# Residual row scale and offset built on chip, first expert tile loaded in halves, router offset first

## The chip, the cores and the metric

One core of a Trainium2 chip. Its engines are TensorE (PE, with its weight loads PEld), VectorE (DVE), ScalarE (ACT), GpSimd (POOL) and SyncE (SP), which here only issues transfers. The metric is the device time of the one core in microseconds, lower is better. A profile of one execution stands beside the timed runs.

## What is computed

A transformer block on 256 tokens of 1024 features, all in float32. Attention (two kinds, gated and merged) is followed by a residual and a layer norm, then 32 experts of which every token uses 4, and a second residual and layer norm.

```python
x = layer_norm(DEEPNORM_ALPHA * x + mix, ln1_g[l], ln1_b[l])     # mix: the attention part
ffn = moe(x.reshape(B * S, D), w_router[l], b_router[l], w_mlp1[l], b_mlp1[l], w_mlp2[l], b_mlp2[l])
x = layer_norm(DEEPNORM_ALPHA * x + ffn.reshape(B, S, D), ln2_g[l], ln2_b[l])

def moe(x2, ...):
    logits = x2 @ w_router + b_router
    top_v, top_i = lax.top_k(logits, 4)
    gates = softmax(top_v)
    # each expert e, on the tokens that chose it
    h = xb @ w_mlp1[e] + b_mlp1[e]                       # 1024 -> 2048
    x_glu, x_lin = minimum(h[:, ::2], 7), clip(h[:, 1::2], -7, 7)
    y = x_glu * sigmoid(1.702 * x_glu) * (x_lin + 1) @ w_mlp2[e] + b_mlp2[e]
```

Every expert's weights are read from DRAM once: 8 MB of `w_mlp1` and 4 MB of `w_mlp2` for each of 32 experts, 402 MB of the 440 MB that the program moves.

## The kernel before, in words

The weights come as chunks of 1 MB, two to a unit. Units 0 to 13 are the attention's weights (28 chunks, `N1` = 28), units 14 to 205 the experts', six to an expert. `seq` is the order in which PE uses them: eight chunks of an expert's first matrix (`m1`), then four of the second matrix of the expert before it (`m2`). A unit lives in a 2 MB tile in SBUF; there are ten places: five of a ring, two of `spl`, one each of `ring4` and `ring3`, and one that is made of two separate 1 MB halves ("nh" and "xl"). SP issues all these loads in program order. When PE has used a chunk, `refill` gives the place to the next unit in `queue`: a 2 MB place is refilled after its second chunk by one transfer (`feed`), the halves one at a time after their own chunk (`feed_half`). Before the experts start, `feed` and `feed_half` fill all ten places while the attention finishes.

Between attention and experts stands the router, in a fixed order that the program writes out (`manual_schedule`): `residual`, `normal` (layer norm), `turn` (transposes of the normed rows to `x1T`), `logits` (eight matmuls with `wr` and one with the offset `br`), `choose` (top 4 on DVE), `count`, `place`, `pick`, then `gather`, which fetches the chosen tokens' rows with matmuls. The first expert chunk follows on PE. Everything later hangs on `at((kind, expert, chunk), f)`: f is issued behind that chunk on each engine that it uses. `combine(e)` adds expert e-2's result to the sums `Y` in PSUM and so frees the buffers "oh" and "ol"; `onehot(e)` spreads an expert's token numbers into the PSUM buffer "pv".

The second residual, ALPHA * x, is added to `Y` by PE: `x1_part` rebuilds x from the normed rows `xn` in quarters (t: half of the tokens, h: half of the features), first times `ln1_g` (j = 0), then plus `ln1_b` (j = 1), and `y_x1` multiplies the quarter by ALPHA times the identity (held in `lstrict` by then). To have g and b in all 128 rows, `x1_load` fetches both with two POOL transfers into the buffer "oh", and a matmul with a broadcast column of `ident` copies one row of it to all rows in "pv". The four quarters are done in experts 3 to 6.

Of the kernel before, what the change touches and what calls it, by code (L numbers as in the profile page):

```python
# [9 lines left out]
F32 = mybir.dt.float32  # L10
# [8 lines left out]
NE = 32  # L19
# [12 lines left out]
def block_kernel(ctx: ExitStack, tc: tile.TileContext, x, xT, w_in, cols_in, b_v, lam_v,  # L32
                 rpbx, w_da, w_na, w_out, ln1_g, ln1_b, w_router, b_router,
                 w1, b1, w2, b2, ln2_g, ln2_b, consts, out):
    nc = tc.nc
# [4 lines left out]
    pp = ctx.enter_context(tc.tile_pool(name="pp", bufs=1, space=bass.MemoryType.PSUM))  # L40

    def act(o, i, f=AF.Copy, **kw):
        return nc.scalar.activation(o, i, f, **kw)  # L43

    def tt(o, a, b, op):
        return nc.vector.tensor_tensor(out=o, in0=a, in1=b, op=op)  # L46
# [17 lines left out]
    N1 = len(chunks)  # L64

    def m1c(e, u):
        return w1[e, u * 256:(u + 1) * 256, :].rearrange("(p r) c -> p r c", p=128)

    def m2c(e, u):
        return w2[e, u * 512:(u + 1) * 512, :].rearrange("(p k) c -> p k c", p=128)  # L70
# [7 lines left out]
    queue = list(range((N1 + len(seq)) // 2))  # L78
    ring = {}
    home = {}  # L80
# [39 lines left out]
    def expert_unit(u):  # L120
        return seq[2 * u - N1]

    half = [None]
    lnt = []

    def feed_half(s):

        if s == 0:
            half[0] = queue.pop(0) if queue else None
        u = half[0]  # L130
        if u is None:
            return
        home[u] = "half"
        kind, e, c = expert_unit(u)
        t = ring[2 * u + s] = big.tile([128, 2048], F32, name="ring5", tag=("nh", "xl")[s])
        if kind == "m1":
            nc.sync.dma_start(t, m1c(e, c // 2)[:, s])
        else:
            nc.sync.dma_start(t.rearrange("p (k c) -> p k c", k=2), m2c(e, c // 2)[:, 2 * s:2 * s + 2])

    def refill(i):

        where = home[i // 2]
        if where == "half":
            feed_half(i % 2)
        elif i % 2:
            if not queue and where is not ring_tile and not lnt:
                load_ln2(where())
            else:
                feed(where)  # L150
# [26 lines left out]
    ident = keep.tile([128, 128], F32, name="ident")  # L177
    lstrict = keep.tile([128, 128], F32, name="lstrict")
    ones = keep.tile([128, 128], F32, name="ones")
# [6 lines left out]
    wr = keep.tile([128, 8, NE], F32, name="wr")  # L186
    br = keep.tile([1, 2, NE], F32, name="br")
# [16 lines left out]
    def at(key, f, *a):  # L204
        after.setdefault(key, []).append((f, a))
# [10 lines left out]
    binT, gcol, g1col, b1col = col[:, 0:40], col[:, 40:41], col[:, 41:49], col[:, 49:57]  # L216
# [10 lines left out]
    p = pp.tile([128, 512], F32, name="tp", bufs=1)  # L227
# [16 lines left out]
    for j in range(4):  # L244
        u, r = divmod(j, 2)
        v = ring[0][:, j * 512:(j + 1) * 512]
# [3 lines left out]
        s = slice(2 * j, 2 * j + 2)  # L250
# [321 lines left out]
    for i in range(N1):  # L572
        if i + 1 < N1:
            split(i + 1)
        if i < 20:
            (proj_v if i // 2 in (2, 5) else proj_t)(i)
        elif i < 24:
            branch(i)
        elif i < 26:
            outproj((i - 24,))  # L580
        elif i == 27:
            outproj((2, 3))
        refill(i)
        if i == N1 - 1:
            feed_half(1)
            for j in range(SPL):
                feed(spl_tile)
        run_after(i)
        if i == 18:

            p1_scope.close()
            p2 = ctx.enter_context(tc.tile_pool(name="p2", bufs=1))
            p2b = ctx.enter_context(tc.tile_pool(name="p2b", bufs=1))
            last = ctx.enter_context(tc.tile_pool(name="last", bufs=1))
            feed(lambda: last.tile([128, 4096], F32, name="ring4"))
        if i == 23:
            feed_half(0)
            feed(lambda: big.tile([128, 4096], F32, name="ring3", tag="qq"))
# [21 lines left out]
    def cut(h):  # L620
        return slice(h * 512, (h + 1) * 512)
# [15 lines left out]
    x1T = big.tile([128, 8, T], F32, name="x1T", tag="xh")  # L637
# [9 lines left out]
    def logits(t):  # L647

        pl = lgs[t] = pp.tile([128, 512], F32, name=("tp", "pv")[t], bufs=1)
        for k in range(8):  # L650
            nc.tensor.matmul(pl[:, 0:NE], lhsT=x1T[:, k, t * 128:(t + 1) * 128], rhs=wr[:, k], start=(k == 0), stop=False)
        nc.tensor.matmul(pl[:, 0:NE], lhsT=ones[0:1], rhs=br[:, 1], start=False, stop=True)

    m8s = {}

# [210 lines left out]

    x1p = []

    def x1_load():

        gb = p2b.tile([4, 512], F32, name="gb", tag="oh", bufs=1)
        for j, src in enumerate((ln1_g, ln1_b)):
            nc.gpsimd.dma_start(gb[2 * j:2 * j + 2], src.rearrange("(h n) -> h n", h=2))
        x1p[:] = [gb, p2b.tile([128, 512], F32, name="x1p", tag="ol", bufs=1)]

    def x1_part(t, h, j):

        p = pp.tile([128, 512], F32, name="pv", bufs=1)
        gb, v = x1p
        nc.tensor.matmul(p, lhsT=ident[0:4, 2 * j + h:2 * j + h + 1].to_broadcast([4, 128]), rhs=gb, start=True, stop=True)  # L880
        tt(v, v if j else xn[:, t, cut(h)], p, ALU.add if j else ALU.mult)

    def y_x1(t, h):

        nc.tensor.matmul(Y[t][:, h], lhsT=lstrict, rhs=x1p[1], start=False, stop=False, skip_group_check=True)  # L885

    yb = []

# [55 lines left out]
    at(("m1", 1, 1), lambda: nc.gpsimd.tensor_scalar(lstrict, ident, ALPHA, None, op0=ALU.mult))  # L944
    for e in range(4):
        t, h = divmod(e, 2)
        at(("m1", e + 3, 1), x1_load)
        at(("m1", e + 3, 3), x1_part, t, h, 0)
        at(("m1", e + 3, 4), x1_part, t, h, 1)
        at(("m1", e + 3, 6), y_x1, t, h)  # L950
    at(("m1", 1, 3), onehot, 0)
    at(("m1", 1, 1), activate, 0)
    at(("m1", 8, 3), y_bias_load)
# [7 lines left out]
    Y = [pp.tile([128, 2, 512], F32, name="pj", bufs=2) for t in range(2)]  # L961
# [5 lines left out]
    residual(1, 1)  # L967
    turn(0)
    logits(0)
    normal(1)  # L970
    choose(0)
    turn(1)
    logits(1)
    count(0)
    choose(1)
# [117 lines left out]
    for t, h in ((1, 1), (0, 0), (0, 1), (1, 0)):  # L1093
        v, y, m = fin[:, t, cut(h)], Y[t][:, h], mv[t]
# [71 lines left out]
```

## Time and profile before

| what | value |
|---|---|
| median of 3 timed runs | 1171.37 us (1169.43 to 1171.55) |
| the profiled execution | 1170.98 us, of which 1169.2 us are the span from its first to its last instruction |
| PE busy | 1085.4 us (93% of the span) |
| DVE, ACT, POOL busy | 369.6, 247.9, 25.2 us |
| mean granted TensorE clock | 0.980 |
| moved by transfers | 439.87 MB, mean 376 GB/s |

The span is told in stretches: up to about 200 us attention, then the router, and from 214 us on the experts. A mean over the span hides that these have different limits, so each sentence below that concerns a stretch uses that stretch's own rows. A PE that is "busy" may be running at half clock, which the column of the granted clock tells.

### The profile page before, as it was taken

The numbers are of one execution on the slowest core, as the hardware profiler recorded it, in microseconds if no ns is written. First come the engines' busy times: TensorE is split into PE (matmuls) and PEld (weight loads), VectorE is DVE, ScalarE is ACT, GpSimd is POOL, SyncE is SP. The second block draws the span as 40 slices with busy tenths as digits, with TensorE's granted clock in tenths as the row PEclk, the third lists the DMA queues.
The fourth block names the chain that finished last, engine by engine and source line by source line (L and its number), as shares of the span: only waits on it lengthen the run. The fifth ranks groups of instructions, "written<-read, shape, count | busy, mean of one in ns | idle before, by whom it ended". The sixth has DMA issues, their size and how long they took to land.

```text
span 1169.2 us, 13431 instructions
## 1 busy us (share of the span) xinstructions
PE 1085.4 (93%) x5592; PEld 522.1 (45%) x5592; DVE 369.6 (32%) x786; ACT 247.9 (21%) x487; POOL 25.2 (2%) x38
## 2 busy tenths in 40 slices
PE   9999999999999999999999999998988998999874
PEld 8887898543332333443433433333333333333221
DVE  6968756132112222222232222222222222222213
ACT  5466843311100111111111111111111111111011
POOL 0001100000000000000000000000000000000001
PEclk9999999899889999999999999999999999999997
DMA  9943469799998899999999999999999999999991
GB/s 337 378 169 113 167 227 369 313 427 426 408 383 354 339 371 411 428 426 427 428 426 428 426 428 425 427 429 427 428 426 425 430 428 426 427 427 429 427 407 51
DMA packets 51043, 439.87 MB, mean 376 GB/s; under 512 B 5906, under 2 KB 9106, under 8 KB 23714
## 3 DMA queue, kind: packets, MB, share of 16 engines
q1 hardware_dynamic: 50098, 437.86, 90.8%
q8 instruction: 46, 0.75, 0.3%
q0 software_dynamic: 592, 0.57, 0.2%
q10 hardware_dynamic: 288, 0.52, 0.1%
q14 instruction: 19, 0.16, 0.0%
HBM read 437.89 MB, written 1.05 MB: 375 GB/s over the span
## 4 chain that ended last, share of the span: by engine, by line
DMA 44%; PE 21%; issue 3%; POOL 0%; POOLq 0%; SPq 0%
DMA ring<-in_w_dram 42%; PE sc L796 10%; PE tp L841 6%; PE sc L815 1%; DMA gb<-in_ln_b_dram 1%; PE tp L731 1%; PE pj L864 1%; PE pv L731 1%; DMA ring<-in_ln_g_dram 0%; PE pv L880 0%; PE pv L760 0%; PE pj L903 0%; PE pj L885 0%; POOLq L1162 0%; POOL ring L1098 0%
## 5 line engine op out<-in xcount | busy, mean ns | idle before, releaser
L796 PE MATMUL sc<-ring,XS 128*64 128x512 f32 x2048 | 482.1, 608 | 33.5 <-DMA ring<-in_w_dram 33.0
L796 PEld LDWEIGHTS sc<-ring,XS 128*64 128x64 f32 x2048 | 138.4, 138 | 307.3 <-issue 254.9
L841 PE MATMUL tp<-ring,hsas 128*64 128x512 f32 x1024 | 234.9, 598 | 14.5 <-DMA ring<-in_w_dram 14.0
L841 PEld LDWEIGHTS tp<-ring,hsas 128*64 128x64 f32 x1024 | 69.1, 136 | 153.6 <-issue 122.5
L804 DVE COPY hsas<-sc 128x512 f32<-128x512 f32 x32 | 22.1, 692 | 310.5 <-PE sc L796 310.5
L43 ACT ACTIVATE XS<-tp,gbx 128x128 f32<-128x128 f32 x64 | 25.8, 453 | 416.7 <-PE tp L731 414.8
L284 PE MATMUL pj<-XH,sp 128*128 128x256 f32 x512 | 96.7, 288 | 4.0 <-DVE sp L46 3.7
L284 PEld LDWEIGHTS pj<-XH,sp 128*128 128x128 f32 x512 | 80.7, 192 | 8.5 <-DVE sp L46 4.9
L46 DVE TENSOR_TENSOR sp<-ring,sp 128x1024 fp32r<-128x1024 f32 (+1 forms) x58 | 68.1, 1188 | 26.9 <-ACT sp L43 26.7
L762 DVE TENSOR_SCALAR GT<-pv,slotp 128x256 fp32r<-128x256 f32 x32 | 15.5, 484 | 186.2 <-PE pv L760 186.2
L284 PE MATMUL pj<-XL,sp 128*128 128x256 f32 x256 | 73.1, 286 | 0.0
L43 ACT ACTIVATE sp<-ring 128x1024 fp32r<-128x1024 f32 (+1 forms) x58 | 58.0, 1023 | 66.9 <-PE pj L284 31.0
L46 DVE TENSOR_TENSOR gl<-sc,bT 128x512 f32<-128x512 f32 x62 | 42.6, 687 | 66.0 <-PE sc L815 66.0
L43 ACT ACTIVATE as<-gl 128x256 f32<-128x256 f32 x64 | 26.7, 416 | 153.7 <-DVE gl L822 153.7
L854 DVE SCALAR_TENSOR_TENSOR ol<-tp,GS,oh 128x512 fp32r<-128x512 f32 x32 | 24.0, 751 | 101.0 <-ACT oh L43 101.0
L284 PEld LDWEIGHTS pj<-XL,sp 128*128 128x128 f32 x256 | 49.2, 192 | 0.6 <-issue 0.6
L43 ACT ACTIVATE oh<-tp,GS 128x512 fp32r<-128x512 f32 x32 | 22.0, 687 | 112.4 <-PE tp L841 112.4
L731 PEld LDWEIGHTS tp<-P,xres 128*128 128x128 f32 x256 | 34.1, 204 | 26.1 <-issue 25.9
L815 PEld LDWEIGHTS sc<-ident,hsas 128*128 128x128 f32 x248 | 32.4, 210 | 25.2 <-issue 25.2
L43 ACT ACTIVATE hsas<-sc 128x512 f32<-128x512 f32 x32 | 19.1, 597 | 103.8 <-PE sc L796 103.8
L731 PE MATMUL tp<-P,xres 128*128 128x128 f32 x256 | 40.3, 303 | 0.1
L815 PE MATMUL sc<-ident,hsas 128*128 128x128 f32 x248 | 38.2, 297 | 0.0
(212 smaller groups left out, 768.3 us busy)
## 6 DMA issues: line engine op xcount, KB each, us to landing
ring<-in_w_dram SPq DMA_DIRECT2D x171, 2048.0 KB, 34.2
ring<-in_w_dram SPq DMA_DIRECT2D x42, 1024.0 KB, 31.9
ring<-in_w_in_dram SPq DMA_DIRECT2D x17, 1024.0 KB, 13.3
ring<-in_w_out_dram SPq DMA_DIRECT2D x4, 1024.0 KB, 6.7
ring<-in_w_in_dram SPq DMA_DIRECT2D x4, 512.0 KB, 7.7
nb<-in_rpbx_dram SPq DMA_DIRECT2D x8, 256.0 KB, 3.6
ring<-in_w_da_dram SPq DMA_DIRECT2D x2, 1024.0 KB, 5.1
ring<-in_w_na_dram SPq DMA_DIRECT2D x2, 1024.0 KB, 7.9
```

The costliest lines, as they stand in the source:

```text
L43: return nc.scalar.activation(o, i, f, **kw)
L46: return nc.vector.tensor_tensor(out=o, in0=a, in1=b, op=op)
L284: nc.tensor.matmul(pj[g][:, c], lhsT=a(k, cc), rhs=b[:, kk], start=(kk == 0 and j == 0 and c % 2 == 0), stop=(kk == 7 and j == 2), skip_gr ...
L731: nc.tensor.matmul(px[:, u], lhsT=v, rhs=P[g][:, t], start=(t == 0), stop=(t == 1))
L762: nc.vector.tensor_scalar(GT[e], p[:, 256:512], slotp[:, 0:1], None, op0=ALU.is_equal)
L796: nc.tensor.matmul(HP[h][j * CAP:(j + 1) * CAP], lhsT=XS[e // 2][:, c, e % 2], rhs=w[:, h, j], start=(c == 0), stop=(c == 7), skip_group_c ...
L804: nc.vector.tensor_copy(HS[e][:, 1], HP[1])
L815: nc.tensor.transpose(p[:, s, k], v[:, s, k], ident)
L841: nc.tensor.matmul(OP[e][j * CAP:(j + 1) * CAP], lhsT=AS[e][:, c, k], rhs=ring[i][:, n:n + 512], start=(c + k == 0), stop=(c == 3 and k == ...
L854: nc.vector.scalar_tensor_tensor(out=ol, in0=OP[e], scalar=GS[e], in1=oh.bitcast(F32), op0=ALU.mult, op1=ALU.subtract)
L864: nc.tensor.matmul(Y[t][:, j], lhsT=GT[e][r, t * 128:(t + 1) * 128], rhs=w[r], start=(e + n == 0), stop=False, skip_group_check=True)
```

## The change

Three edits. The residual's quarters move from experts 3 to 6 to experts 9 to 12, with other places inside the expert, and g and b reach all rows without transfers: ACT multiplies the identity by a column of g (or b) that has been in SBUF since the start, four times for 512 features, and a matmul with a matrix of ones sums each column of that diagonal. Unit 14, the first that the experts use, goes to the two halves instead of unit 18, which takes a full place. In the router the offset's matmul comes ahead of the eight others, and two matmuls of ones, whose result nobody reads, are put behind the first offset.

```diff
-    half = [None]
+    half = [N1 // 2]
+    queue.remove(N1 // 2)
...
-        if s == 0:
+        if s == 0 and N1 // 2 in home:
             half[0] = queue.pop(0) if queue else None
...
         pl = lgs[t] = pp.tile([128, 512], F32, name=("tp", "pv")[t], bufs=1)
+        nc.tensor.matmul(pl[:, 0:NE], lhsT=ones[0:1], rhs=br[:, 1], start=True, stop=False)
+        if t == 0:
+            keep_clock(2)
         for k in range(8):
-            nc.tensor.matmul(pl[:, 0:NE], lhsT=x1T[:, k, t * 128:(t + 1) * 128], rhs=wr[:, k], start=(k == 0), stop=False)
-        nc.tensor.matmul(pl[:, 0:NE], lhsT=ones[0:1], rhs=br[:, 1], start=False, stop=True)
+            nc.tensor.matmul(pl[:, 0:NE], lhsT=x1T[:, k, t * 128:(t + 1) * 128], rhs=wr[:, k], start=False, stop=(k == 7))
+
+    def keep_clock(n):
+
+        p = pp.tile([128, 512], F32, name="sc", bufs=2)
+        for j in range(n):
+            nc.tensor.matmul(p[:, 0:128], lhsT=ones, rhs=ones, start=True, stop=True)
...
-    def x1_load():
-
-        gb = p2b.tile([4, 512], F32, name="gb", tag="oh", bufs=1)
-        for j, src in enumerate((ln1_g, ln1_b)):
-            nc.gpsimd.dma_start(gb[2 * j:2 * j + 2], src.rearrange("(h n) -> h n", h=2))
-        x1p[:] = [gb, p2b.tile([128, 512], F32, name="x1p", tag="ol", bufs=1)]
-
     def x1_part(t, h, j):
 
+        gb = p2b.tile([128, 4, 128], F32, name="gb", tag="oh", bufs=1)
+        for k in range(4):
+            act(gb[:, k], ident, scale=(g1col, b1col)[j][:, 4 * h + k:4 * h + k + 1])
         p = pp.tile([128, 512], F32, name="pv", bufs=1)
-        gb, v = x1p
-        nc.tensor.matmul(p, lhsT=ident[0:4, 2 * j + h:2 * j + h + 1].to_broadcast([4, 128]), rhs=gb, start=True, stop=True)
+        nc.tensor.matmul(p, lhsT=ones, rhs=gb.rearrange("p k c -> p (k c)"), start=True, stop=True)
...
-        at(("m1", e + 3, 1), x1_load)
-        at(("m1", e + 3, 3), x1_part, t, h, 0)
-        at(("m1", e + 3, 4), x1_part, t, h, 1)
-        at(("m1", e + 3, 6), y_x1, t, h)
+        at(("m1", 9 + e, 2), x1_part, t, h, 0)
+        at(("m1", 9 + e, 4), x1_part, t, h, 1)
+        at(("m1", 9 + e, 6), y_x1, t, h)
```

PE in the first expert that has a quarter, expert 3 before. L796 are the expert's chunks (four rows each), L760 is `onehot`, L880 the copy of g or b to all rows, L731 `gather`, L885 `y_x1`:

```order
L796 MATMUL sc<-ring,XS 64x512 x8
L864 MATMUL pj<-oh,GT 128x512 x4
L864 MATMUL pj<-ol,GT 128x512 x4
L796 MATMUL sc<-ring,XS 64x512 x4
L760 MATMUL pv<-rows,stack 128x512
L796 MATMUL sc<-ring,XS 64x512 x4
L880 MATMUL pv<-gb,ident 128x512
L796 MATMUL sc<-ring_2415,XS 64x512 x4
L880 MATMUL pv<-gb,ident 128x512
L796 MATMUL sc<-ring_2415,XS 64x512 x4
```

The same place now, in expert 9 (L805 the chunks, L769 `onehot`, L884 the copy):

```order
L805 MATMUL sc<-ring,XS 64x512 x8
L873 MATMUL pj<-oh,GT 128x512 x4
L873 MATMUL pj<-ol,GT 128x512 x4
L805 MATMUL sc<-ring,XS 64x512 x4
L769 MATMUL pv<-rows,stack 128x512
L884 MATMUL pv<-gb,ones 128x512
L805 MATMUL sc<-ring,XS 64x512 x8
L884 MATMUL pv<-gb,ones 128x512
L805 MATMUL sc<-ring,XS 64x512 x4
```

The first copy has come forward by one chunk: it now stands right behind `onehot`, which writes the same buffer "pv"; the second keeps its place, two chunks behind the first instead of one. On ACT eight builds of "gb" stand between `gate_o` (oh) and the gather's evictions (XS) of each of these four experts:

```order
L43 ACTIVATE oh<-tp,GS 128x512
L43 ACTIVATE gb<-ident,col 128x128 x8
L43 ACTIVATE XS<-tp,gbx 128x128 x2
L43 ACTIVATE XS<-pv,gbx 128x128 x2
L43 ACTIVATE hsas<-sc 128x512
```

Before, ACT went there from `oh` to `XS` at once. In the router PE had, before (L644 `turn`, L651 the eight matmuls, L652 the offset, L680 and L679 `count`):

```order
L644 MATMUL sc<-ident,xres 128x128 x8
L651 MATMUL tp<-wr,x1T 128x32 x8
L652 MATMUL tp<-br,ones 128x32
L644 MATMUL sc<-ident,xres 128x128 x8
L651 MATMUL pv<-wr,x1T 128x32 x8
L652 MATMUL pv<-br,ones 128x32
L680 MATMUL sc<-maskM,lstrict 128x32
```

and has now (L651 the offset, L661 the two matmuls of ones, L655 the eight):

```order
L645 MATMUL sc<-ident,xres 128x128 x8
L651 MATMUL tp<-br,ones 128x32
L661 MATMUL sc<-ones 128x128 x2
L655 MATMUL tp<-wr,x1T 128x32 x8
L645 MATMUL sc<-ident,xres 128x128 x8
L651 MATMUL pv<-br,ones 128x32
L655 MATMUL pv<-wr,x1T 128x32 x8
L689 MATMUL sc<-maskM,lstrict 128x32
```

Each offset has moved ahead of its eight matmuls, and two matmuls stand between the first offset and the first eight.

## Rows read from the trace of the kernel before

**Rows 1.** Windows; stretch, its length, busy us by engine, granted clock, transfers' share, GB/s

```profile
230.00:300.00 70.00, 67.72 (x336) 27.19 (x330) 18.89 (x48) 10.50 (x23) 1.11 (x2) 1.00 1.01 426
300.00:440.00 140.00, 131.93 (x544) 47.45 (x546) 30.80 (x70) 14.91 (x32) 2.98 (x6) 0.90 0.92 368
440.00:600.00 160.00, 160.00 (x790) 63.98 (x788) 39.23 (x95) 23.50 (x50) 2.01 (x4) 1.00 1.01 424
600.00:800.00 200.00, 189.66 (x933) 75.32 (x931) 44.46 (x109) 27.70 (x60) 0.00 (x0) 1.00 1.01 428
```

**Rows 2.** Windows of 5 us in the same view, two of the stretch 300 to 440

```profile
350.00:355.00 5.00, 5.00 (x22) 1.36 (x18) 0.69 (x1) 0.60 (x1) 0.00 (x0) 1.00 0.21 52
...
420.00:425.00 5.00, 5.00 (x23) 1.76 (x22) 0.69 (x1) 0.60 (x1) 0.00 (x0) 1.00 0.82 279
```

**Rows 3.** Waits of PE; for whom, us in total, times, longest us

```profile
PE sc L796 <- DMA ring<-in_w_dram: 33.0, 30, 1.6
...
PE pv L880 <- DMA gb<-in_ln_b_dram: 10.0, 4, 2.7
```

**Rows 4.** Timeline of expert 3; start, length, instructions, [idle before, on whom]

```profile
295.69 0.49 PE L760 MATMUL pv<-rows,stack 96*128 96x512 f32 x1
...
296.23 0.48 DVE L762 TENSOR_SCALAR GT<-pv,slotp 128x256 fp32r<-128x256 f32 x1 [5.31 <-PE pv L760]
296.75 0.42 DVE L765 SCALAR_TENSOR_TENSOR as<-GT,pv 128x256 f32<-128x256 f32 x1
...
300.61 2.04 PE L880 MATMUL pv<-gb,ident 4*128 4x512 f32 x2 [2.55 <-DMA gb<-in_ln_b_dram]
302.58 3.68 PE L796 MATMUL sc<-ring,XS 128*64 128x512 f32 x8
...
307.63 1.94 PE L796 MATMUL sc<-ring,XS 128*64 128x512 f32 x8
```

**Rows 5.** Chain of work that ended last; start, length, what

```profile
408.25 1.09 PE pv L880 x2
...
419.73 1.05 PE pj L885 x2
...
514.93 1.13 PE pj L864 x8
...
540.93 1.13 PE pj L864 x8
...
615.54 35.57 DMA ring<-in_w_dram
```

**Rows 6.** Groups by line; busy us, mean ns of one, idle before

```profile
L43 ACT ACTIVATE XS<-tp,gbx 128x128 f32<-128x128 f32 x64 | 25.8, 453 | 416.7 <-PE tp L731 414.8 <-issue 1.7
```

**Rows 7.** Timeline of SP's issues at the start of the experts

```profile
219.32 7.52 SPq L113 DMA_DIRECT2D ring<-in_w_dram  x2
...
226.51 7.74 SPq L113 DMA_DIRECT2D ring<-in_w_dram  x3
```

**Rows 8.** Windows of 5 us at the router's end and the first chunks

```profile
210.00:215.00 5.00, 4.87 (x22) 3.62 (x24) 1.07 (x7) 1.58 (x6) 0.54 (x1) 0.52 1.01 433
215.00:220.00 5.00, 5.00 (x28) 2.44 (x25) 0.00 (x0) 0.80 (x2) 0.00 (x0) 1.00 0.07 30
225.00:230.00 5.00, 5.00 (x26) 1.66 (x24) 2.73 (x16) 3.61 (x8) 0.00 (x0) 1.00 0.73 246
```

**Rows 9.** Timeline of PE in the router and at the first gathers

```profile
202.66 1.97 PE L651 MATMUL tp<-wr,x1T 128*128 128x32 f32 x16 [0.31 <-ACT x1T L43]
...
208.18 0.63 PE L652 MATMUL pv<-br,ones 1*128 1x32 f32 x2
...
211.22 2.05 PE L731 MATMUL tp<-P,xres 128*128 128x128 f32 x8
...
213.86 2.41 PE L796 MATMUL sc<-ring,XS 128*64 128x512 f32 x8
...
216.20 1.21 PE L731 MATMUL pv<-P,xres 128*128 128x128 f32 x8
```

More of the change, by code (lines that the diff above doesn't have):

```diff
@@ L867, in block_kernel @@
     x1p = []
-    def x1_load():
-        gb = p2b.tile([4, 512], F32, name="gb", tag="oh", bufs=1)
-        for j, src in enumerate((ln1_g, ln1_b)):
-            nc.gpsimd.dma_start(gb[2 * j:2 * j + 2], src.rearrange("(h n) -> h n", h=2))
-        x1p[:] = [gb, p2b.tile([128, 512], F32, name="x1p", tag="ol", bufs=1)]
     def x1_part(t, h, j):
+        gb = p2b.tile([128, 4, 128], F32, name="gb", tag="oh", bufs=1)
+        for k in range(4):
+            act(gb[:, k], ident, scale=(g1col, b1col)[j][:, 4 * h + k:4 * h + k + 1])
         p = pp.tile([128, 512], F32, name="pv", bufs=1)
-        gb, v = x1p
-        nc.tensor.matmul(p, lhsT=ident[0:4, 2 * j + h:2 * j + h + 1].to_broadcast([4, 128]), rhs=gb, start=True, stop=True)
+        nc.tensor.matmul(p, lhsT=ones, rhs=gb.rearrange("p k c -> p (k c)"), start=True, stop=True)
+        if j == 0:
+            x1p[:] = [p2b.tile([128, 512], F32, name="x1p", tag="ol", bufs=1)]
+        v = x1p[0]
         tt(v, v if j else xn[:, t, cut(h)], p, ALU.add if j else ALU.mult)
     def y_x1(t, h):
-        nc.tensor.matmul(Y[t][:, h], lhsT=lstrict, rhs=x1p[1], start=False, stop=False, skip_group_check=True)
+        nc.tensor.matmul(Y[t][:, h], lhsT=lstrict, rhs=x1p[0], start=False, stop=False, skip_group_check=True)
     yb = []
```

## The prediction, made before the run

> **What bounds the kernel now.** I start with stretches, because the busy shares of the whole span mislead here: PE is 93% busy, yet it isn't PE alone that sets the end. From 230 to 300 us the transfers run at 426 GB/s, from 440 on at 424 and 428 [rows 1]; 427 is what this program gets when a load is always outstanding. Between 300 and 440 they make only 368, although 32 experts' weights are still waiting to be read, with windows as low as 52 GB/s [rows 1, 2]. The loads can't run ahead there: all ten places are full, and a place becomes free only when PE has used it. So in that stretch PE's delays turn into idle time of the transfers, and idle transfers are never made up, since from 440 to the end they run at their full rate.
>
> After 440 PE is ahead of what the transfers can follow. Two equal points of neighbouring experts are 540.93 - 514.93 = 26.0 us apart [rows 5]; an expert's 12 MB (12.58 million bytes) take 29.45 us at 427 GB/s. PE uses up the stock in the places, 3.45 us per expert, and PE's chain ends at 615.54, where its first wait for a weight begins [rows 5]. From there on the transfers alone set the time; PE's waits for weights (33.0 us at the expert's first matrix, 30 times, 1.6 at most) are theirs [rows 3].
>
> Why is PE late from 300 to 440? Its waits name one thing apart from weights: L880, the copy of g and b, 10.0 us in 4 waits [rows 3]. Expert 3 shows one. `onehot` and the next chunk are done by 298.1, then PE stands 2.55 us for the second POOL transfer, and after that it runs at half its speed: eight chunk matmuls take 3.68 us, later 1.94 again [rows 4]. From the first such copy (300.61) to the fourth (408.25) it is 107.6 us, 35.9 per expert [rows 4, 5], 9.9 more than 26.0: 2.5 of waiting, 3.2 of the quarter's own matmuls at full speed (1.09, as much again, and 1.05 for y_x1 [rows 5]) and about 4.2 of half clock.
>
> **Does this lag explain the lost transfer time?** By bytes the loss is 140 x (1 - 368/427) = 19.3 us. By the lag: places were last full at the release of 226.51 [rows 7]; until 295 PE gained 69 x (1 - 26.0/29.45) = 8 us of stock, then lost 4 x (35.9 - 29.45) = 25.8, so 17.8 us of idle. The two roads agree within 1.5 us. I take the bytes, since they are counted, and 17.8 to 19.6 (with 428) for the range.
>
> **The residual's quarters.** Removed are eight small POOL transfers and PE's four waits for them. With the quarters gone from experts 3 to 6, those experts cost 26.0 us like the later ones, less than the 29.45 of the transfers, so the transfers have no idle time left there: -19.3.
>
> What comes back in experts 9 to 12? Eight builds of a 128x128 tile on ACT: nothing of before builds from SBUF with a column as scale, the nearest is the gather's eviction, 128x128 with a column of scale and of offset, 0.45 us [rows 6]; nothing to 0.45 each, I take 0.45. Four make 1.8 us. They can start when `combine` has read "oh", and one chunk (1.94 [rows 4]), `onehot` and its DVE work lie beside them: hidden, and if that cover were gone, 1.8 us of PE wait per copy. Behind them on ACT stand only the gather's evictions, three chunks later. The matmul with ones has 512 columns as before and costs the same 1.09 as the copy from four rows; y_x1, which already has 128 rows, shows 1.05 [rows 5]. New is the wait behind `onehot`: the copy writes "pv", which DVE reads until 297.17, while `onehot` itself ended at 296.18 [rows 4], so PE stands 1.0 us. The second copy is two chunks on, past the DVE work, and waits for nothing.
>
> So such an expert takes 26.0 + 3.2 + 1.0 = 30.2 us, 0.8 more than the transfers need; even if each wait drew the same 4.2 us of half clock, 34.4. PE waited up to 1.6 us for weights [rows 3] and the windows from 440 to 800 still show the clock at 1.00 [rows 1], so I take 30.2. What covers it is the stock. Emptied from the last window below rate, 425 [rows 2], to 615.54 [rows 5], it is 190 x (1 - 26.0/29.45) = 22 us, less some 2 for the second matrix's offset in expert 8: about 20. In the new run it starts full at 226.5 and is empty near 410, so experts 9 to 12 may lose 20 us before a transfer idles. Forecast 4 x 0.8 = 3, with half clock 20: **cost 0**.
>
> **The first tile in halves.** The first refill of before goes out at 219.32, when both chunks of unit 14 are used; the next at 226.51 [rows 7]. Between, the transfers are empty, almost wholly from 215 to 220 and partly from 225 to 230 [rows 8]. With halves 1 MB goes out one chunk and one gather earlier, near 216. That moves idle time and doesn't remove it: the next place is freed at 226.51 as before, and by then both megabytes have long landed in either case. The last point at which everything waits for PE is that release, and it doesn't move: **0**. At most it could be worth the 3 us by which the load is earlier, if the windows behind 226.5 didn't run full; they do, at 426. The halves now come up first instead of fifth, with the same number of 1 MB loads.
>
> **The router.** Its length moves the release of 226.51 one for one. The offset of the second half is 0.63 us at the end of the eight matmuls [rows 9] and now lies in the gap before them, where PE waits for ACT: -0.6. The two matmuls of ones wait for the eviction that frees "sc", as the eight did; eight 128-column instructions take 1.21 us at full clock [rows 9], four of them 0.6, from nothing if they hide in the 0.31 of waiting to 0.6 if they don't. The first offset leaves the path and gives some 0.3 back. Sum -0.6 + 0.6 - 0.3 = **-0.3**. That leaves the clock. It is at 0.52 from 210 to 215 [rows 8], and there a gather takes 2.05 us instead of 1.21 and the first chunk 2.41 instead of 1.94 [rows 9]; with the small matmuls of `count` some 1.7 us. If the two matmuls keep the clock up, -1.7 more. They stand near 203, seven microseconds ahead of that window, with small matmuls and short gaps between, so I take it that they don't, not firmly.
>
> On the clock the Trainium skill, "TensorE: Matmul & The Clock Gate" (Part 1), says that the throttled state is the default and that activity releases it. By that rule extra matmuls can hold the clock, and the sum would have the further -1.7; the trace bears out that the clock goes after a gap at L880, but no run here shows what two matmuls do in the router.
>
> **Sum.** The profiled execution took 1170.98 us, 0.4 below the median of the three. 1170.98 - 19.3 - 0.3 = **1151.4 us**.
>
> **The rivals.**
> *The clock holds in the router* (0.27): the release of 226.51 comes 1.7 us earlier still, 1149.7. For it speaks that the slow stretch is short and the first eight matmuls still ran at full pace (1.97 us [rows 9]); against it that everything behind the two matmuls stays as it was.
> *The transfers don't reach 427 when PE runs without stops* (0.10): then 300 to 440 is limited by its rate, in part or whole. At 409 in that stretch the gain is 140 x (1 - 368/409) = 14 us: 1157. Against it: 230 to 300 has the same mix without the quarters, at 426 [rows 1]. The extreme is that 368 is the limit there, so that the change does nothing (0.03): 1171. "DMA: Bandwidth & Descriptors" of the Trainium skill (Where 436 GB/s comes from) puts the limit of loads from HBM at about 358 GB/s per core, by which nothing could be won; here 424 to 428 over 360 us [rows 1] say otherwise.
> *Experts 9 to 12 become the new stop* (0.04), the one that ends slower. If PE, after its wait behind `onehot`, fell to half clock and stayed there, an expert would take about twice 26 + 4 us. The transfers start to idle when four experts lose over 20 us, and the gain is eaten at 20 + 19.6 = 39.6: 29.45 + 9.9 = 39.4 us per expert, 13 above 26.0. At 56 us it would be 4 x 26.5 - 20 = 86 of idle, 1151 + 86 = 1237. Against it: the quarters of before, with 2.5 us of waiting, came to 35.9 and the clock recovered in each of them [rows 4].
>
> **How the numbers follow.** The forecast itself has 0.56: 1150.5 to 1153.5 by the bounds of the lag and of the two matmuls. The range takes in the holding clock with the upper bound of the gain (1149) and the middle of the lower transfer rate: 1148 to 1158, which leaves out some 0.15. A measurement of this kernel can tell about 0.2%, 2.3 us, from no change. Faster: 0.56 + 0.27 + 0.10 = 0.93; within: 0.03; slower: 0.04.
>
> **What the profile will show.** Right: no window under 415 GB/s between 230 and 440, apart from the first; no wait of PE on a transfer of g or b; experts 3 to 6 26 us each; the first wait of PE for a weight near 410 instead of 615; in experts 9 to 12 a wait of about 1.0 us before L884, on DVE. The first load of the experts goes out near 216, and the second release still near 226, at most 0.5 us earlier unless the window 210 to 215 shows the clock at 1.00. Wrong: windows at half rate that come back between 460 and 600, which means that the stock is smaller than 20 us or L884 waits far longer; or full stock and a rate below 420 between 300 and 440.

## The result

The changed kernel takes 1152.29 us (median of 4 runs, 1150.53 to 1153.78) beside 1170.4 us on the same chip: a ratio of 0.9846, with a 95% interval of 0.9825 to 0.9868. Its profiled execution took 1151.79 us, 1149.7 of them its span; 1151.4 was forecast, against the profiled execution of before (1170.98), so the profiled execution gained 19.2 us where 19.6 was said; the medians differ by 18.1 us.

The stretches of the profile after, which answer to [rows 1]:

```profile
230.00:300.00 70.00, 69.67 (x346) 28.08 (x344) 18.88 (x48) 10.68 (x24) 0.00 (x0) 1.00 1.00 425
300.00:440.00 140.00, 140.00 (x697) 56.74 (x695) 33.08 (x80) 21.66 (x47) 2.08 (x4) 1.00 1.01 424
440.00:600.00 160.00, 155.47 (x727) 59.22 (x725) 42.22 (x97) 30.75 (x76) 0.00 (x0) 1.00 1.01 427
600.00:800.00 200.00, 187.44 (x919) 73.66 (x917) 44.45 (x109) 26.12 (x56) 0.00 (x0) 1.00 1.01 427
```

From 300 to 440 us PE is busy throughout, its clock is at 1.00 instead of 0.90, and the transfers make 424 GB/s where they made 368. The 56 GB/s over 140 us are 18.4 us at 427 GB/s; 440 to 600 brings 1.1 more, 427 after 424, and the second release of the experts (the second time that a used place goes back to the loads) came 0.8 later; half a microsecond of the 19.2 stays unassigned. The 424 in 300 to 440 is one dip: from 420 to 425 us the transfers make 338 GB/s, though PE is busy throughout and they are too (their share is 0.99). Just ahead, from 417.80, POOL issues four transfers of 64 KB, which fetch the second matrix's offset in expert 8. Before, the same four were issued from 454.53, and 460 to 465 made 338. So the dip only changed rows, and the two gains belong together: 19.5 us. From 600 on nothing differs but the moment at which it happens.

PE's waits after, to [rows 3]:

```profile
PE sc L805 <- DMA ring<-in_w_dram: 31.1, 27, 2.1
PE tp L850 <- DMA ring<-in_w_dram: 11.7, 15, 1.3
PE pv L884 <- DVE as L774: 4.5, 4, 1.1
```

The 10.0 us for the transfers of g and b are gone. The new wait behind `onehot` is there, on DVE, 1.1 us each. Expert 9 in the timeline, to [rows 4]:

```profile
452.66 0.63 PE L873 MATMUL pj<-ol,GT 64*128 64x512 f32 x4
452.87 1.28 ACT L43 ACTIVATE gb<-ident,col 128x128 f32<-128x128 f32 x4 [3.34 <-PE pj L873]
...
453.22 1.94 PE L805 MATMUL sc<-ring,XS 128*64 128x512 f32 x8
...
455.09 0.50 PE L769 MATMUL pv<-rows,stack 96*128 96x512 f32 x1
455.63 0.48 DVE L771 TENSOR_SCALAR GT<-pv,slotp 128x256 fp32r<-128x256 f32 x1 [5.31 <-PE pv L769]
456.14 0.42 DVE L774 SCALAR_TENSOR_TENSOR as<-GT,pv 128x256 f32<-128x256 f32 x1
...
456.72 1.10 PE L884 MATMUL pv<-gb,ones 128*128 128x512 f32 x2 [1.13 <-DVE as L774]
...
457.75 3.65 PE L805 MATMUL sc<-ring,XS 128*64 128x512 f32 x16
```

ACT has its four builds done in 1.28 us while PE works on the next chunk, so they end 2.6 us before L884 starts: PE waits for DVE's second reader of "pv" alone. Behind the wait the 16 matmuls of two chunks take 3.65 us, full clock. Before, the eight of one chunk took 3.68 [rows 4].

### The profile page after: what moved, and what is told of

Its sections match the earlier page's. It is cut to its first block, busy times and chain, and to the rows that moved or that the text cites. A ratio compares the mean times of both kernels' runs of the same rounds, so it can differ in the third digit from the quotient of the medians.

```text
span 1149.7 us, 13448 instructions
## 1 busy us (share of the span) xinstructions
PE 1071.6 (93%) x5596; PEld 518.7 (45%) x5596; DVE 370.6 (32%) x786; ACT 258.3 (22%) x519; POOL 21.3 (2%) x30
## 4 chain that ended last, share of the span: by engine, by line
DMA 45%; PE 44%; issue 4%; DVE 3%; ACT 2%; SPq 0%; POOL 0%; POOLq 0%; ACTq 0%
DMA ring<-in_w_dram 43%; PE sc L805 17%; PE tp L850 8%; PE pj L285 5%; PE pj L469 2%; PE tp L740 2%; PE sc L824 1%; PE pv L740 1%; DMA ring<-in_w_in_dram 1%; PE pj L873 1%; PE pj L300 1%; PE sc L510 1%; DVE tm L46 1%; ACT sp L43 1%; PE pv L884 1%
## 5 line engine op out<-in xcount | busy, mean ns | idle before, releaser
L805 PE MATMUL sc<-ring,XS 128*64 128x512 f32 x2048 | 473.7, 600 | 34.9 <-DMA ring<-in_w_dram 31.1
L805 PEld LDWEIGHTS sc<-ring,XS 128*64 128x64 f32 x2048 | 137.8, 137 | 305.0 <-issue 250.0
L740 PEld LDWEIGHTS tp<-P,xres 128*128 128x128 f32 x256 | 33.4, 200 | 24.6 <-issue 24.3
L824 PEld LDWEIGHTS sc<-ident,hsas 128*128 128x128 f32 x248 | 32.3, 210 | 25.2 <-issue 25.2
L740 PE MATMUL tp<-P,xres 128*128 128x128 f32 x256 | 39.4, 298 | 0.1
```

What stands on the lines that cost most here:

```text
L740: nc.tensor.matmul(px[:, u], lhsT=v, rhs=P[g][:, t], start=(t == 0), stop=(t == 1))
L805: nc.tensor.matmul(HP[h][j * CAP:(j + 1) * CAP], lhsT=XS[e // 2][:, c, e % 2], rhs=w[:, h, j], start=(c == 0), stop=(c == 7), skip_group_c ...
L824: nc.tensor.transpose(p[:, s, k], v[:, s, k], ident)
```

## The experiments

All kernels of one group ran on one chip beside the kernel before, whose medians there were 1171.99 (first four), 1170.82 (next four) and 1172.81 us (last four). Times are medians where a ratio to that median stands, with its 95% interval in brackets, and one run where none does.

**The quarters alone** (halves and router as before).

> Only the residual's quarters are changed (on chip, experts 9 to 12); halves and router as before. Theory (the whole gain is the transfers' idle time that the quarters' stops caused in experts 3 to 6): the ratio to before is that of the full change, 0.984 to 0.985, some 1152 us, and 300 to 440 us runs at 424 GB/s or more. Rival (a part of the gain comes from the earlier refill through the halves, up to 3 us, or from the router): 1153.5 to 1156 us.

1154.14 us, ratio 0.9851 (0.982 to 0.9882); 300 to 440 at 423 GB/s. It is the whole change within the interval, as the theory has it, and the stretch runs as forecast. The time itself lies where the rival had it, and the interval, 1151 to 1158 us, holds both; what the halves and the router are worth is therefore read from the runs that have them alone.

**The quarters only moved, with their transfers.**

```diff
-        at(("m1", e + 3, 1), x1_load)
-        at(("m1", e + 3, 3), x1_part, t, h, 0)
...
+        at(("m1", 9 + e, 1), x1_load)
+        at(("m1", 9 + e, 3), x1_part, t, h, 0)
```

> The quarters keep their POOL transfers and are only moved to experts 9 to 12. Theory (a stop costs only what the stock of loaded weights can't cover): each such expert takes 35.9 us as before, 6.4 more than its transfer, 26 in four; the changed kernel's stock at expert 9 is about 23 us, so 3 us of idle at most, between 560 and 590 us: 1152 to 1156. Rival (the waits on the small transfers cost the same wherever they stand): 1170.

1155.13 us, ratio 0.9856 (0.9829 to 0.9884). This is the run that separates the two readings of the old waits. Its waits of PE and its windows, 440 to 600:

```profile
PE pv L880 <- DMA gb<-in_ln_b_dram: 9.3, 4, 2.8
```

```profile
440.00:600.00 160.00, 150.67 (x633) 53.21 (x631) 36.95 (x85) 17.04 (x36) 4.01 (x8) 0.91 1.01 427
600.00:800.00 200.00, 200.00 (x998) 80.37 (x993) 49.21 (x121) 29.85 (x64) 0.00 (x0) 1.00 1.01 427
```

The four waits are all there, 9.3 us, and so is the half clock, 0.91 on the mean; yet the transfers run at 427 on the mean of both stretches, and the time is that of the changed kernel within the interval. So the eight small transfers don't slow the weights' by themselves either. In experts 3 to 6 the same waits cost the 17 us that this run gains. The 3 us of idle that I allowed for did not show: from one y_x1 to the next (474.37 to 579.69, three experts) an expert took 35.1 us, and 4 x (35.1 - 29.45) = 22.6 us of lag stayed covered.

**The quarters on chip, but in experts 3 to 6** at their old chunks, `x1_load` taken out.

> The quarters are built on chip but stay in experts 3 to 6, at their old chunks 3 and 4. Theory: without the 2.5 us wait the clock stays up, an expert takes 26.0 + 3.2 = 29.2 us, less than the 29.45 of its transfers, so no idle time: 1151 to 1153. Rival (the place is what matters, since 3 experts after the start there is hardly any stock): some of the idle time stays, 1157 to 1165.

1155.09 us, ratio 0.9859 (0.9826 to 0.9892), 2 us over what was expected, which the interval (1152 to 1159) doesn't tell apart. The stretch decides, full clock and 427 GB/s (the dip of the offset's transfers lies past 440 here, 326 GB/s from 440 to 445):

```profile
300.00:440.00 140.00, 140.00 (x650) 52.84 (x648) 36.02 (x82) 27.59 (x68) 2.08 (x4) 1.00 1.01 427
```

So the other half of the edit is enough by itself as well: 3 us of quarter per expert fit beside the transfers, the stop with its half clock didn't. How much of the old cost is the wait and how much the half clock behind it, no run separates. Building on chip and moving are two cures for one cost, and with both the second has nothing left to win.

**The first tile in halves alone.**

> Only unit 14 in halves; quarters and router as before. Theory: worth nothing, 1169 to 1172, since the release that binds is that of the second tile, near 226.5; the first 1 MB goes out near 216 and 225 to 230 is emptier than before. Rival (the earlier megabyte is 2.4 us of transfer time won): 1167 to 1168.5.

1171.47 us, ratio 0.9996 (0.9975 to 1.0017): nothing. The issues of SP, in the one profile, agree with the reason that was given:

```profile
219.17 3.49 SPq L138 DMA_DIRECT2D ring<-in_w_dram  x2
229.53 7.74 SPq L113 DMA_DIRECT2D ring<-in_w_dram  x3
```

The two halves go out at 219.2 and 222.3 and the next place is free at 229.5, 10.4 us after the first half; from 225 to 230 the transfers make 128 GB/s where they made 246 [rows 8]. Only a part of that drop is the earlier megabyte: this profile's release came 3.0 us later than the 226.51 of before, since the slow stretch of the clock was longer here (last section). That the halves are worth nothing rests on the timed runs.

**The router's part alone.**

> Only the router's part: offsets first and the two matmuls of ones. Theory (worth less than can be measured: 0.6 us of offset saved, some 0.7 us of dummies added, and the slow stretch of the clock only begins later): 1169 to 1172, ratio within 0.998 to 1.002. Rival (the clock stays up and 1.7 us are won): ratio 0.998 or less, windows 205 to 220 at a clock of 1.00.

1170.15 us, ratio 0.9992 (0.9963 to 1.0022): not measurable. The clock is at 0.50 from 210 to 215 all the same.

**Without the two matmuls of ones**, otherwise the changed kernel.

```diff
-        if t == 0:
-            keep_clock(2)
```

> The changed kernel without the two matmuls of ones. Theory: the same time within 0.7 us, 1151 to 1153; the clock falls about two microseconds earlier, at the count's matmuls, as before. Rival (the dummies hold something up that matters): 1154 or more.

1151.07 us, ratio 0.9832 (0.9805 to 0.9859). The time is as expected; the clock is not. It didn't fall at the matmuls of `count` (0.39 us): the first gather still took 1.18 us, and only the first chunk was slow (3.40).

**Four more matmuls of ones**, ahead of the second half's eight.

```diff
-        if t == 0:
-            keep_clock(2)
+        keep_clock((2, 4)[t])
```

> The changed kernel with four more matmuls of ones, ahead of the second half's eight logit matmuls. If activity shortly ahead of the fall keeps the clock: the first gather takes 1.2 instead of 2.05 us and the first chunk 1.9 instead of 3.6, less some 0.7 for the dummies: the second release near 225.5 instead of 227.3, 1150.5. If it falls all the same: 0.7 later, 1153.

1152.29 us, ratio 0.9845 (0.9816 to 0.9874). The first gather kept its full speed (1.18 us), but the first chunk then ran slowly (3.62): the slow stretch began later and did not go. That the four matmuls moved it is not shown, since without any matmuls of ones the same two rows took 1.18 and 3.40. The second release came at 226.72, neither at 225.5 nor 0.7 later than 227.3.

**Each quarter fetched and rebuilt twice** in experts 9 to 12, with transfers, halves and router as before. The lines that it has beyond the quarters only moved:

```diff
+        at(("m1", 9 + e, 6), x1_load)
+        at(("m1", 9 + e, 7), x1_part, t, h, 0)
+        at(("m2", 8 + e, 0), x1_part, t, h, 1)
```

> The quarters keep their transfers in experts 9 to 12 and each is fetched and rebuilt a second time, for nothing, later in the same expert. Theory (stops cost nothing until the stock is used up, and after that one for one): such an expert takes 44 to 47 us, 15 to 17 more than its transfers, 58 to 70 in four; the stock is at least the 26 that the single stops used without idle, some 30: the transfers idle for 30 to 40 us between 480 and 590, 1182 to 1192, slower than before the change. Rival (work off the transfers' path is always hidden there): 1155.

1157.12 us, one run: a miss in size. The second fetch went out early and PE never waited for it, so that an expert took 37.4 us (first copies at 458.42 and 570.75, three experts apart) and not 45. Over 60 us the transfers lost 60 x (1 - 388/427) = 5.5 us:

```profile
560.00:620.00 60.00, 57.37 (x252) 21.10 (x250) 13.96 (x32) 6.88 (x16) 1.99 (x4) 0.94 0.96 388
```

Four experts lose 4 x (37.4 - 29.45) = 32 us to their transfers, of which 5.5 come out as idle. As time they show only roughly: from the second release to the end of the span it is 929.3 us, 923.6 with the quarters only moved, and 922.4 to 926.2 in the profiles of the changed kernel, its versions with other matmuls of ones and the one without quarters. By the idle time, then, at expert 9 there were some 26 us to lose.

**Plain PE work in the same place**, 60 unused matmuls in each of experts 9 to 12.

```diff
+        at(("m1", 9 + e, 5), pad, 60)
```

> The changed kernel with 60 more matmuls of ones, unused, in each of experts 9 to 12: some 17 us of PE work each, no waits. Theory (PE's lag there costs nothing until the stock is used up, then one for one): such an expert takes 47.5 us, 18 more than its transfers, 72 in four; the doubled stops used 36 with 5.6 of idle, so the stock is some 30: idle 42, 1194, with windows far below 427 GB/s between 510 and 600. With the stock of 20 that the prediction worked with: 1204. Rival (hidden): 1152.

1192.29 us, one run, 39 more than the changed kernel on the same chip and slower than the kernel before. The stretch where it happened, and the next:

```profile
520.00:660.00 140.00, 135.94 (x770) 70.71 (x768) 26.79 (x62) 18.43 (x44) 0.00 (x0) 1.00 0.76 312
660.00:800.00 140.00, 140.00 (x698) 56.56 (x698) 32.71 (x81) 20.26 (x44) 0.00 (x0) 1.00 1.01 428
```

An expert took 45.2 us (the padding starts at 465.62 and 510.82), 63 us more than the transfers in four; idle by bytes is 140 x (1 - 312/427) = 37.7, so about 25 us were hidden. The clock stays at 1.00, and from 440 to 660 PE waits for no transfer: neither such a wait nor a slow clock is needed. What counts is how long PE keeps the places, and the cost is one for one once the stock is gone.

**Without the quarters** (ALPHA * x left out, so the result lacks a term; the run is for the time alone).

> The changed kernel without the residual's quarters: ALPHA * x is left out of the second residual. Theory (in experts 9 to 12 the quarters cost nothing): 1151 to 1153 as the changed kernel; PE's first wait for a weight comes when the stock of some 30 us is used, after expert 9, near 500 instead of 591. Rival (they still cost something): 1148 or less.

1153.31 us, one run, no faster than the changed kernel (1153.22 on this chip): in experts 9 to 12 the quarters are free, as far as one run can tell. The "591" of the expectation is a transfer's row in the chain, as the 615.54 of the prediction is; the changed kernel's first wait for a weight stands behind 680. Here it is, in the timeline:

```profile
517.26 1.94 PE L850 MATMUL tp<-ring,hsas 128*64 128x512 f32 x8 [0.70 <-DMA ring<-in_w_dram]
```

**The changed kernel and the one without dummies on one chip.**

> The changed kernel once more, beside the same without the two matmuls of ones. From the router's first transpose to the second release of the experts it took 25.3 to 25.6 us in three profiles with the two matmuls, 25.2 to 28.2 in six with the old router. Theory (the two matmuls keep the slow stretch from starting early): 25.3 to 25.6 again, 1151 to 1152.5.

> The changed kernel without the two matmuls of ones, again, on the same chip as the changed kernel itself. If the two matmuls keep the slow stretch short: 25 to 28 us from the first transpose to the second release, and 1152 to 1154. If they only cost their 0.7 us: 24.0 to 24.9 as in the first profile, 1151.

1153.22 us (0.9839, 0.9814 to 0.9863) and 1152.05 us (0.9819, 0.9796 to 0.9842). From the first transpose to the second release they took 24.3 and 23.8 us. The stretch missed both expectations, 25.3 to 25.6 and 24.0 to 24.9, by 1.0 and 0.2 us. The intervals overlap, so that the version without the two matmuls is not shown to be faster, only not slower in two trials, and 0.5 us shorter in this stretch. It has the lowest ratios of those I ran.

## Why the prediction was right, step by step

*The lag from 300 to 440 is the loss.* Held. The gain by bytes in that stretch is 18.4 us, and with the dip that moved into it from the next one 19.5, for the 19.3 forecast. That the old stops cost only there is shown from two sides: the waits kept but moved (1155), the place kept but the waits removed (1155). That it is PE's lateness and not the wait as such is shown by plain work, which costs in the later place too once it is long enough (1192). One sign failed in its letter: of the 5 us windows between 235 and 440 four lie under 415, at 400, 413, 413 and 338 GB/s. PE is busy throughout from 300 on, and the one that is far below is the dip of the offset's transfers.

*Experts 9 to 12 at 30.2 us, cost 0.* They take 30.6 (the chain's second-matrix rows), wait 1.1 as against 1.0, ACT builds 0.39 apiece against 0.45. The cost is 0 by the run without quarters, within its one time.

```profile
443.43 5.30 PE tp L850 x24
...
474.08 5.30 PE tp L850 x24
...
504.72 5.30 PE tp L850 x24
```

*The stock.* Here a step failed, without harm to the sum. I had it "empty near 410", from PE's chain "ending" at 615.54. That row is a transfer, from its issue on, and no wait of PE; PE's first wait for a weight stood between 680 and 690, before the change and after it alike. So the stock lasts far longer. Without quarters it is empty at 517: PE had then used 132 chunks since the second release, at 225.28 in that profile, 138.4 million bytes, and the transfers, at a mean of 423 GB/s over these 292.0 us, had brought 123.5. The whole stock is 14.9 MB, some 35 us of transfer, not 22. What was needed for the forecast was another quantity, how much of it is used up when expert 9 begins and so can be lost again: "about 20" was said, and the doubled stops and the padding give 25 to 26. The count that the prediction made up to 295 would have come closer: from 227.3 to expert 9 at 452.7 it gives 225.4 x (1 - 26.0/29.45) = 26.4, less 2.6 for expert 8 (28.6 us from 414.81 to 443.43 in the chain), so some 24, an estimate. The price at which the place turns slower than before was put at 39.4 us per expert; with 25 it is 29.45 + (25 + 19.6) / 4 = 40.6, and the padding at 45.2 lies beyond it and did come out slower than before.

*Halves 0.* Held: the first half went out at 217.1, and the release that binds came at 227.3, both about a microsecond later than said.

```profile
217.11 3.33 SPq L138 DMA_DIRECT2D ring<-in_w_dram  x2
227.30 0.33 SPq L113 DMA_DIRECT2D ring<-in_w_dram  x1
```

*Router -0.3, clock falls all the same.* The sign was wrong by a little in this pair of profiles: from the first transpose (201.76 after, 201.31 before) to the second release it took 25.5 us against 25.2. The term that was mis-sized is the clock. I took the slow stretch as it stood in one profile; it moves, to where it costs more:

```profile
203.10 0.71 PE L661 MATMUL sc<-ones 128*128 128x128 f32 x4
...
208.50 0.39 PE L689 MATMUL sc<-maskM,lstrict 128*128 128x32 f32 x2
...
210.84 2.05 PE L740 MATMUL tp<-P,xres 128*128 128x128 f32 x8
...
213.48 3.59 PE L805 MATMUL sc<-ring,XS 128*64 128x512 f32 x8
```

`count` is at full speed now (0.39), the first gather still slow, and the first chunk takes 3.59 us where it took 2.41 [rows 9]. The two matmuls took 0.55 us up to the start of the next (203.65), near the upper bound of 0.6.

*The rivals.* The clock did not hold in any run: 210 to 215 shows 0.50 to 0.79 in every profile. The transfers reach 424 to 427 when PE doesn't stop, so neither 409 nor 368 was a limit of theirs. By the 358 GB/s of the Trainium skill ("DMA: Bandwidth & Descriptors", Where 436 GB/s comes from), taken as a limit on this core, no gain was possible; the trace disagrees, 424 to 427 GB/s on the mean of each stretch from 230 to 800.

## What to carry to other kernels

Where loads run ahead of an engine through a fixed number of places, a stop of that engine costs what the stock of used-up places can't take back: put side work where the stock has been drawn down, not where the places are still full, and removing its waits matters only in the second case. The stock has an end: here some 25 us of lag were free, and what went beyond them was paid in full. Two cures for the same stop don't add; ask what is late after the first. A place freed earlier gains nothing if the next release still finds the transfers empty: look for the last release at which they wait.

## What the runs showed that I had not expected

The slow stretch of TensorE's clock in the router begins at no fixed instruction. With the router of before, six profiles took 25.2, 28.1, 26.9, 28.1, 28.2 and 25.2 us from the first transpose to the second release; with the halves alone it began at the second eight matmuls:

```profile
206.21 3.62 PE L652 MATMUL pv<-wr,x1T 128*128 128x32 f32 x16 [0.21 <-ACT x1T L43]
```

3.62 us instead of the 2.0 of the first profile. With the offset first, six profiles with two or more matmuls of ones took 25.5, 25.3, 25.6, 24.3, 24.3 and 24.3, two without them 24.0 and 23.8. The new order may therefore be worth a microsecond or two and the matmuls of ones nothing, but these are single profiles on several chips, and the timed run of the router's part alone doesn't show it. That stays open.
